# Splitting the last third of the modulation product: its gate half is multiplied during the expert routing, and its weights lead the experts' load queue

## The chip, the cores and the metric

The kernel runs on one core of one Trainium2 chip. Its time is the device time of one execution in microseconds (us). Five engines run side by side on the core: PE does the matrix products, DVE and ACT the elementwise work, POOL little here, and SP issues almost all loads from device memory. Each engine takes its instructions strictly in the order in which they were written for it, and waits on semaphores for the others.

## The reference

The kernel computes two transformer blocks over 256 tokens of width 1024 in fp32. What matters here is the first block and its modulation vector, six pieces of 1024 numbers that all come from one small product:

```python
cond = jax.nn.silu(c)                      # (1, 1024)
mod = cond @ mod_w[l] + mod_b[l]           # (1, 6144)
shift1, scale1, gate1, shift2, scale2, gate2 = jnp.split(mod, N_MOD, axis=-1)
h = modulate(rms_norm(x, norm1_g[l]), shift1, scale1)
x = x + gate1[:, None, :] * mixer_sublayer(h, ...)
h = modulate(rms_norm(x, norm2_g[l]), shift2, scale2)
x = x + gate2[:, None, :] * hierarchical_moe(h, ...)
```

`mod_w` is 1024 x 6144, 24 MiB in fp32. `scale2` is needed as soon as the mixer's last product begins (it goes into the router's weights); `gate2` only where the experts' results are added to x. `hierarchical_moe` gives each token two of 32 experts (1024 to 2 x 256 and back to 1024).

## The kernel before, in words

**Loads.** Weights come in chunks of 1 MiB (128 x 2048 fp32), each issued by SP into a slot of a ring. The mixer's ring has six slots (`load`, L264 to 269). The experts' chunks have a queue of their own, `self.order` (L477): 8 blocks of 4 experts, each with 8 chunks `egu` (gate and up) and 4 chunks `edn` (down). `issue` (L280) takes from that queue into the slots of `eslots` in turn: nine (`ring2`), issued at L852 in the mixer's gate product, five (`ring3`) and the mixer's six, issued during its last product, and three (`ring4`) at L996 in the routing. So 23 expert chunks can be on the chip before the experts begin; the next load has to wait until a slot has been read (`weights`, L288, hands the chunks out in the same order).

**The modulation.** `mod` (L491) multiplies one such chunk at a time: `csil`, the 1024 conditions as 8 columns, is spread to 32 columns and is the stationary operand, and the weights stream past, in four strips of 32 output partitions. `modcols` (L525) copies the sums to SBUF on ACT, turns them with PE transposes, and adds the bias on DVE into `modc`, 48 columns of 128. The first third (`mod0`) is multiplied at the start. The middle third (`mod1`) is done on DVE (`modsum`). The last third, `mod2` (scale2 and gate2, 8 chunks, one per block of 128 conditions, W = 512), is multiplied inside the first part of the input projection: `win_a` (L633) calls `self.pump(2)` (L644) for each of its output tiles from the fourth chunk on, and each call issues a load and then the 4 matmuls of that chunk.

**The rest of the path.** Most weights are split in two parts in fp32r on ACT (`whi`, L300) and DVE (`wlo`, L301), and PE multiplies three products of these (L316, L317, L321). After the mixer, `moe` (L930) turns x with transposes (L950), scales it on ACT (L951, `hn`), and finds each token's experts in a chain of small DVE steps (L968 to 985). Two groups of small matmuls (L989 to 992) count the positions, DVE makes the gather matrices `Ph` (L1063), and PE gathers the tokens (L1072) and multiplies them by the first `egu` chunks (L1089). In the middle of the experts there is one runtime branch (`overflow`, L1247), before which SP has to have issued all loads that stand ahead of it.

The order of each engine's instructions is not the order of the source alone: the program is built by a scheduler that simulates the engines and places each instruction when its operands are due, and pools of buffers make a later writer wait for the earlier reader.

Of the kernel before, what the change touches and what calls it, by code (L numbers as in the profile page):

```python
# [13 lines left out]
F32 = mybir.dt.float32  # L14
# [7 lines left out]
P = 128  # L22
T = 256
D = 1024
KD = D // P
# [3 lines left out]
NE = 32  # L29
# [103 lines left out]
def arrange(x, c, mod_w, mod_b, norm1_g, w_in, conv_w, conv_b, igate_b, fgate_b, q_norm_g, kv_norm_g,  # L133
# [10 lines left out]
    a = {}  # L144
# [2 lines left out]
    half = np.concatenate([np.r_[512 * j:512 * j + 512, 1024 + 512 * j:1536 + 512 * j] for j in range(2)])  # L147
    a["mod0"] = mod_w[0][:, half].reshape(4, 2, P, 2, 1024).transpose(3, 0, 2, 1, 4).reshape(8, P, 2048)
    a["mod1"] = mod_w[0][:, 2048:4096].reshape(KD, P, 2048)
    a["mod2"] = mod_w[0][:, 4096:].reshape(KD, P, 2048)  # L150
    tl = _tiles(p1)
    a["win_a"] = _group(tl, 2)
    a["win_v"] = np.concatenate([_kblk(w1[:, 1024 + 512 * j:1536 + 512 * j], 4) for j in range(2)])
# [69 lines left out]
class Prog:  # L223
# [239 lines left out]
    def run(self, stop=None):  # L463
        tc, nc, I = self.tc, self.nc, self.I
        v, a, g, te = nc.vector, nc.scalar, nc.gpsimd, nc.tensor
        es = ExitStack()
        with es:
            keep = self.pool(es, "keep", 1)
            xT = keep.tile([P, KD, T], F32, name="xT")
            self.const(keep, "first", ["c", "modb", "n1"], nc.sync)  # L470
            nc.sync.dma_start(xT, I["xT"].rearrange("p (k t) -> p k t", k=KD))
            self.const(keep, "tab0", ["ident", "ones", "sel32"], nc.sync)
            modc = keep.tile([P, 48], F32, name="modc")
            cols = keep.tile([P, 64], F32, name="cols")
            self.ring = self.pool(es, "ring", RING1)
            self.eslots, self.eloads, self.ahead = [], 0, []
            self.order = [x for b in range(NE // 4 - 1) for x in self.chunks(b)]  # L477
            self.xT, self.modc, self.cols, self.keep = xT, modc, cols, keep
            with ExitStack() as em:
                self.mixer(em)  # L480
                self.dump("x1", xT)
                if stop == 1:
                    return
                self.moe()
            self.dump("x2", xT)
            if stop == 2:
                return
            self.block2()


    def mod(self, t0, W, src, psum, pool, load=None):  # L491

        nc = self.nc
        ps = psum("md", 1)
        kb = 512 // W
        for ch in range(KD // kb):
            w = (load or self.load)(src(ch))
            yield
            for i in range(kb):
                k = ch * kb + i  # L500
                for j in range(4):
                    nc.tensor.matmul(ps[32 * j:32 * j + 32, :W], self.csil[:, k:k + 1].to_broadcast([P, 32]),
                                     w[:, i * 4 * W + j * W:i * 4 * W + (j + 1) * W], start=k == 0, stop=k == KD - 1)
            yield
        self.modcols(ps, t0, W, psum, pool)

    def modsum(self, t0, name, acc, psum, pool):

# [13 lines left out]
            nc.tensor.matmul(ps[32 * j:32 * j + 32, :], self.co("ones", 0, 32), acc[:, j * 512:(j + 1) * 512], start=True, stop=True)  # L522
        self.modcols(ps, t0, 512, psum, pool)

    def modcols(self, ps, t0, W, psum, pool):  # L525
        nc = self.nc
        row = pool.tile([P, 512], F32, name="mrow", tag="yf", bufs=1)
        nc.scalar.copy(row[:, :W], ps[:, :W])
        nq = W // P
        tmp = psum("md", 1)  # L530
        for q in range(nq):
            nc.tensor.transpose(tmp[:, q * P:(q + 1) * P], row[:, q * P:(q + 1) * P], self.co("ident"))
        nc.vector.tensor_tensor(
            out=self.modc[:, t0:t0 + 4 * nq].rearrange("p (j q) -> p q j", q=nq),
            in0=tmp[:, :W].rearrange("p (q j r) -> p q j r", q=nq, j=4)[:, :, :, 0],
            in1=self.co("modb", t0, 4 * nq).rearrange("p (j q) -> p q j", q=nq), op=OP.add)
# [10 lines left out]
    def mixer(self, em):  # L547
        tc, nc, I = self.tc, self.nc, self.I
        v, a, g, te = nc.vector, nc.scalar, nc.gpsimd, nc.tensor
        mm = te.matmul  # L550
        xT, modc, cols = self.xT, self.modc, self.cols
        with ExitStack() as eo:
# [4 lines left out]
            ps = self.pool(eo, "ps1", 1, space=PSUM)  # L557
# [9 lines left out]
            with ExitStack() as ei:  # L567
                pa = self.pool(ei, "pa", 1)
                tm = self.pool(ei, "tm", 2)
# [32 lines left out]
                for j in range(2):  # L602
# [6 lines left out]
                    for i in range(4):  # L609
                        k = 4 * j + i  # L610
# [3 lines left out]
                                               op0=OP.add, op1=OP.subtract)  # L614
                        a.activation(hf[:, k], hf[:, k], AF.Identity, bias=sh[:, i:i + 1])
                macc = pa.tile([P, 2048], F32, name="macc")
                self.later = [self.mod(32, 512, lambda k: I["mod2"][k], psum, tm), self.modsum(16, "mod1", macc, psum, tm)]

                craw = pa.tile([P, 5, T], F32, name="craw", tag="ce")
                krz = [pa.tile([P, T], F32, name=f"krz{i}") for i in range(2)]  # L620
# [6 lines left out]
                def win_a(ch):  # L627
                    w = self.load(I["win_a"][ch]) if ch else w0
                    if ch == 2:
                        self.const(pa, "trig", ["cos", "sin", "cosq", "sinq"], nc.sync)  # L630
                    if ch == 3:
                        self.const(self.keep, "small", ["n2", "cw", "cb", "qg", "kvg", "fg", "n12", "n22", "b2", "pe", "cw2",
                                                        "cb2"], nc.sync)  # L633
                    if ch == 6:
                        self.const(self.keep, "tab", ["ustrict", "sel64", "riota", "iota"], nc.sync)
                        self.const(pa, "wif", ["wif"], nc.sync)
                        self.rows(self.keep, "row1", ["ib", "fb", "bg", "br"])
                        self.const(pa, "tri", ["negu", "cmask"], nc.sync)
                    pp = psum("a", 2)
                    for j in range(2):  # L640
                        n = ch * 2 + j
                        o = pp[:, j * T:(j + 1) * T]
                        if ch > 2:
                            self.pump(2)  # L644
                        self.tile_a(w[:, j * 1024:(j + 1) * 1024], h, [(o, 0, KD)])
                        if n < 5:
                            a.copy(craw[:, n], o)
                            i = n // 3
                            self.sumsq1(parts[i], craw[:, n], n - 3 * i, groups[i][1], tm)
                        elif n == 5:  # L650

                            kr1 = tm.tile([P, T], F32, name="kr1", tag="x", bufs=5)
                            kr2 = tm.tile([P, T], F32, name="kr2", tag="x", bufs=5)
                            lo, up = slice(0, 64), slice(64, 128)
                            for i, r in ((0, lo), (1, up)):
                                v.tensor_tensor(out=kr1[r], in0=o[lo], in1=self.co("cos")[lo], op=OP.mult)
                                v.tensor_tensor(out=kr2[r], in0=o[up], in1=self.co("sin")[up], op=OP.mult)
                                v.tensor_tensor(out=krz[i][r], in0=kr1[r], in1=kr2[r], op=OP.add)
                        else:

                            c = n - 6
                            xp = tm.tile([P, T + 3], F32, name="xp", tag="x", bufs=5)
                            g.memset(xp[:, 0:3], 0.0)
                            a.copy(xp[:, 3:], o)
                            ca = tm.tile([P, T], F32, name="ca", tag="x", bufs=5)
                            a.activation(ca, o, AF.Identity, scale=self.co("cw", 24 + c, 1), bias=self.co("cb", c, 1))
                            for d in range(3):
                                v.scalar_tensor_tensor(out=ca, in0=xp[:, d:d + T], scalar=self.co("cw", d * 8 + c, 1),
                                                       in1=ca, op0=OP.mult, op1=OP.add)
                            th = tm.tile([P, T], F32, name="th", tag="x", bufs=5)  # L670
                            a.activation(th, ca, AF.Tanh, scale=0.5)
                            v.scalar_tensor_tensor(out=conv[:, c], in0=th, scalar=1.0, in1=ca, op0=OP.add, op1=OP.mult)
# [40 lines left out]
                for ch in range(3):  # L713
                    w = self.load(I["uq"][ch])
                    for j in range(4):
                        n = ch * 4 + j
# [14 lines left out]
                w = self.load(I["uk"][0])  # L731
# [6 lines left out]
                w = self.load(I["uv"][0])  # L738
# [13 lines left out]
                for hd in range(8):  # L752
# [5 lines left out]
                    x = self.softmax(S, Pn, sm)  # L758
# [14 lines left out]
                for c in range(2):  # L773
                    outs = [psum("a", 2) for _ in range(2)]
                    for hf2 in range(2):
                        w = self.load(I["win_v"][c * 2 + hf2])
# [33 lines left out]
                for ch in range(4):  # L810
                    w = self.load(I["win_og"][ch])
# [6 lines left out]
                for hd in range(4):  # L818
# [19 lines left out]
                    yf = tm.tile([P, 2, T], F32, name="yf", tag="yf", bufs=1)  # L838
# [9 lines left out]
            for ch in range(8):  # L848
                w = self.load(I["win_og"][4 + ch])
# [78 lines left out]
    def moe(self):  # L928
# [4 lines left out]
        with ExitStack() as eo:  # L933
# [4 lines left out]
            def psum(tag, bufs):  # L938
                return ps.tile([P, 512], F32, name="ps_" + tag, tag=tag, bufs=bufs)
# [6 lines left out]
            for q in range(2):  # L946
                for j in range(2):
                    o = psum("x", 2)
                    for i in range(4):
                        te.transpose(o[:, i * P:(i + 1) * P], xT[:, j * 4 + i, q * P:(q + 1) * P], self.co("ident"))  # L950
                    a.activation(hn[:, q, j * 512:(j + 1) * 512], o, AF.Copy, scale=rsc[:, q:q + 1])  # L951


            def b2(x, n):
# [871 lines left out]
```

## Time and profile before

| | |
|---|---|
| median of 3 runs | 1007.67 us (1006.49 to 1008.81) |
| the profiled execution | 1006.2 us, span 1004.4 us |
| PE busy | 928.5 us, 92% of the span |
| DVE, ACT busy | 604.9 us, 473.3 us |
| read from device memory | 247.49 MB |

The span is from the first to the last instruction in the trace; 1.8 us of the execution lie around it. Averages say little here, since the stages have different limits: the first 88 us, the mixer up to 326 us, the routing from 326 to 344 us, the experts to about 550 us, and the second block. A stretch is read by asking which engine or queue has no idle time in it, and, where none is full, who waited for whom. PE clock 1.00 is 2.4 GHz, 0.50 is 1.2 GHz.

### The profile page before, as it was taken

What the parts mean: (1) busy time and instruction counts of PE and PEld (TensorE: products, weight loads), DVE (VectorE), ACT (ScalarE), POOL (GpSimd) and SP (SyncE); (2) the same over time, 40 slices, a digit from 0 to 9 for tenths busy, and PEclk for the clock granted to TensorE, in tenths of its full rate; (3) what the DMA queues carried; (4) which work ended last, traced back from release to release, by engine and by line L of the source; (5) the groups of instructions that cost most, each with busy time, mean ns of one, the idle gap of its engine ahead of it and who ended that gap; (6) DMA issues with size and microseconds to landing.
All of it is one profiled execution on the core that took longest, in us unless ns stands there. A gap on an engine that the chain in (4) does not pass through costs nothing. (4 is left out here: it accounts for less than half of the span.)

```text
span 1004.4 us, 17784 instructions
## 1 busy us (share of the span) xinstructions
PE 928.5 (92%) x6870; PEld 761.9 (76%) x6870; DVE 604.9 (60%) x1463; ACT 473.3 (47%) x1006; POOL 13.0 (1%) x28
## 2 busy tenths in 40 slices
PE   4899899999999899997698999899998999999995
PEld 2678888999999545443232898788898889999994
DVE  2468699664663524223123884787769687676764
ACT  3546866555443122121112765476754565555553
POOL 0000000000000000000000000000001000000001
PEclk9899899999999799998989999999999999999998
DMA  8977367669558599999989654643245344555501
GB/s 358 408 275 283 123 243 264 248 233 421 223 204 355 196 420 416 413 422 418 418 344 421 250 189 149 250 152 137 92 169 189 126 169 168 193 185 174 205 1 43
DMA packets 37387, 249.76 MB, mean 249 GB/s; under 512 B 4272, under 2 KB 5040, under 8 KB 8368
## 3 DMA queue, kind: packets, MB, share of 16 engines
q1 hardware_dynamic: 37008, 248.01, 64.0%
q8 instruction: 56, 0.92, 0.4%
q10 hardware_dynamic: 288, 0.55, 0.2%
q14 instruction: 35, 0.29, 0.1%
HBM read 247.49 MB, written 1.05 MB: 247 GB/s over the span
## 5 line engine op out<-in xcount | busy, mean ns | idle before, releaser
L301 DVE TENSOR_TENSOR wlo<-w,whi 128x512 fp32r<-128x512 f32 (+2 forms) x426 | 287.9, 683 | 152.8 <-ACT whi L300 137.5
L300 ACT CAST whi<-w 128x512 fp32r<-128x512 f32 (+2 forms) x426 | 257.7, 611 | 253.1 <-PE ps_a L317 195.2
L316 PE MATMUL ps_a<-hh,whi 128*128 128x256 f32 x304 | 79.1, 292 | 4.9 <-ACT hh L612 3.1
L317 PE MATMUL ps_a<-hl,whi 128*128 128x256 f32 x304 | 78.5, 289 | 0.0
L1132 DVE SCALAR_TENSOR_TENSOR xT<-ps_c,modc,xT 128x256 f32<-128x256 f32 x72 | 33.1, 483 | 72.7 <-PE ps_c L1131 72.6
L316 PE MATMUL ps_a<-h4h,whi 128*128 128x256 f32 x304 | 76.1, 283 | 0.2 <-ACT h4h L343 0.2
L317 PE MATMUL ps_a<-h4l,whi 128*128 128x256 f32 x304 | 76.1, 283 | 0.0
L1089 PE MATMUL ps_gu<-w,xg 128*32 128x512 f32 x512 | 68.7, 618 | 6.5 <-issue 6.5
L316 PEld LDWEIGHTS ps_a<-hh,whi 128*128 128x128 f32 x304 | 59.4, 196 | 9.1 <-ACT hh L612 3.3
L316 PE MATMUL ps_a<-h2h,whi 128*128 128x256 f32 x248 | 64.2, 289 | 0.5 <-DVE kn L1509 0.5
L317 PE MATMUL ps_a<-h2l,whi 128*128 128x256 f32 x248 | 63.0, 284 | 0.0
L317 PEld LDWEIGHTS ps_a<-hl,whi 128*128 128x128 f32 x304 | 59.6, 196 | 2.0 <-issue 1.2
L316 PEld LDWEIGHTS ps_a<-h4h,whi 128*128 128x128 f32 x304 | 58.1, 192 | 1.2 <-ACT h4h L343 0.6
L317 PEld LDWEIGHTS ps_a<-h4l,whi 128*128 128x128 f32 x304 | 58.2, 192 | 0.3
L1131 PE MATMUL ps_c<-PT,eo 128*128 128x256 f32 (+1 forms) x144 | 41.9, 410 | 13.1 <-ACT eo L1137 12.1
L1131 PEld LDWEIGHTS ps_c<-PT,eo 128*128 128x128 f32 (+1 forms) x144 | 24.3, 192 | 37.3 <-ACT eo L1137 16.4
L1072 PEld LDWEIGHTS ps_x<-Ph,hn 128*128 128x128 f32 x256 | 34.0, 198 | 22.4 <-issue 17.6
L321 PE MATMUL ps_a<-hh,wlo 128*128 128x256 f32 x304 | 49.9, 288 | 0.3 <-DVE wlo L301 0.3
L316 PEld LDWEIGHTS ps_a<-h2h,whi 128*128 128x128 f32 x248 | 47.4, 191 | 2.9 <-issue 1.8
L321 PE MATMUL ps_a<-h4h,wlo 128*128 128x256 f32 x304 | 48.7, 283 | 0.0
L1077 ACT ACTIVATE xg<-ps_x,modc,cols 128x128 f32<-128x128 f32 x32 | 14.6, 457 | 70.4 <-PE ps_x L1072 60.9
L317 PEld LDWEIGHTS ps_a<-h2l,whi 128*128 128x128 f32 x248 | 47.4, 191 | 0.2 <-issue 0.2
(527 smaller groups left out, 1998.5 us busy)
## 6 DMA issues: line engine op xcount, KB each, us to landing
w<-in_egu_dram SPq DMA_DIRECT2D x66, 1024.0 KB, 18.4
w<-in_edn_dram SPq DMA_DIRECT2D x33, 1024.0 KB, 19.8
w<-in_up_dram SPq DMA_DIRECT2D x22, 1024.0 KB, 4.7
w<-in_w2a_dram SPq DMA_DIRECT2D x20, 1024.0 KB, 6.6
w<-in_mod_dram SPq DMA_DIRECT2D x19, 1024.0 KB, 7.0
w<-in_win_og_dram SPq DMA_DIRECT2D x12, 1024.0 KB, 5.9
w<-in_dn_dram SPq DMA_DIRECT2D x11, 1024.0 KB, 4.8
w<-in_br_dram SPq DMA_DIRECT2D x8, 1024.0 KB, 12.5
```

Of the source, the lines that this page charges most:

```text
L300: nc.scalar.copy(hi, src)
L301: nc.vector.tensor_tensor(out=lo, in0=src, in1=hi.bitcast(F32), op=OP.subtract)
L316: mm(out, hi[:, s], ah[:, k], start=first, stop=False)
L317: mm(out, hi[:, s], al[:, k], start=False, stop=False)
L321: mm(out, lo[:, s], ah[:, k], start=False, stop=last)
L1072: mm(o[:, i * P:(i + 1) * P], hn[:, q, d * P:(d + 1) * P], Phs[b][q], start=q == 0, stop=q == 1)
L1077: a.activation(xgs[0][:, i], o[:, i * P:(i + 1) * P], AF.Identity, scale=ac[:, d:d + 1], bias=modc[:, 24 + d:25 + d])
L1089: mm(gu[32 * j:32 * j + 32], xgs[d // 4][:, d % 4, j * CAP:(j + 1) * CAP], w[:, j * 512:(j + 1) * 512], start=d == 0, stop=d == KD - 1)
L1131: mm(o[:, i * T:(i + 1) * T], eo_[:, (d0 + i) * P:(d0 + i + 1) * P], PT, start=True, stop=True)
L1132: v.scalar_tensor_tensor(out=xT[:, d], in0=o[:, i * T:(i + 1) * T], scalar=g2[:, d:d + 1], in1=xT[:, d], op0=OP.mult, op1=OP.add)
```

## The change

The weights of `mod2` are cut in two. Four chunks with scale2's 1024 columns stay where they were, now two blocks of conditions to a chunk and W = 256. Four chunks `mod3` with gate2's columns become the first four entries of the experts' queue, and are multiplied in `moe` behind the transposes of x, with a sum in one of the two `dn` banks and a row buffer of the experts' `eo` tag.

```diff
-    a["mod2"] = mod_w[0][:, 4096:].reshape(KD, P, 2048)
+    for n, c0 in (("mod2", 4096), ("mod3", 5120)):
+        a[n] = mod_w[0][:, c0:c0 + 1024].reshape(4, 2, P, 1024).transpose(0, 2, 1, 3).reshape(4, P, 2048)
...
-            self.order = [x for b in range(NE // 4 - 1) for x in self.chunks(b)]
+            self.order = [[(lambda w: w, I["mod3"][k])] for k in range(4)]
+            self.order += [x for b in range(NE // 4 - 1) for x in self.chunks(b)]
...
-    def mod(self, t0, W, src, psum, pool, load=None):
+    def mod(self, t0, W, src, psum, pool, load=None, tag="yf", bufs=1):
...
-        row = pool.tile([P, 512], F32, name="mrow", tag="yf", bufs=1)
+        row = pool.tile([P, 512], F32, name="mrow", tag=tag, bufs=bufs)
...
-                self.later = [self.mod(32, 512, lambda k: I["mod2"][k], psum, tm), self.modsum(16, "mod1", macc, psum, tm)]
+                self.later = [self.mod(32, 256, lambda k: I["mod2"][k], psum, tm), self.modsum(16, "mod1", macc, psum, tm)]
...
-                            self.pump(2)
+                            self.pump()
...
                     a.activation(hn[:, q, j * 512:(j + 1) * 512], o, AF.Copy, scale=rsc[:, q:q + 1])
+            for _ in self.mod(40, 256, lambda k: k, lambda *_: psum("dn", 2), tm, lambda _: self.weights(), "eo", 2):
+                pass
```

Line numbers of the changed kernel are 2 higher from its L150 on, 4 higher from the queue and 8 higher behind the new loop. What moves can be seen at three places. On PE in the input projection, where the second group of the last third's matmuls stands (ps_md is their bank, ps_a the projection's), before and now:

```order
L321 MATMUL ps_a<-hh,wlo 128x256 x4
L502 MATMUL ps_md<-w,csil 32x512 x10
L382 MATMUL ps_m<-tab_62,sqs 128x1 x4
L316 MATMUL ps_a<-hh,whi 128x256
L317 MATMUL ps_a<-hl,whi 128x256
```

```order
L323 MATMUL ps_a<-hh,wlo 128x256 x4
L506 MATMUL ps_md<-w,csil 32x256 x10
L384 MATMUL ps_m<-tab_62,sqs 128x1 x4
L506 MATMUL ps_md<-w,csil 32x256
L318 MATMUL ps_a<-hh,whi 128x256
L319 MATMUL ps_a<-hl,whi 128x256
```

The 32 matmuls stay in this stage with half as many columns; they stood in groups of 6, 10, 8 and 8, and stand in groups of 6, 10, 1 and 15.

On PE in the routing (ps_x holds x turned, ps_dn the new sum, ps_c the positions), before and now:

```order
L904 MATMUL ps_m<-tab_62,sq 128x1 x2
L950 MATMUL ps_x<-tab_62,xT 128x128 x16
L989 MATMUL ps_c<-oh,tab 128x32 x2
L991 MATMUL ps_c<-oh,tab_62 128x32
L992 MATMUL ps_c<-oh,tab 128x32
L991 MATMUL ps_c<-oh,tab_62 128x32
L992 MATMUL ps_c<-oh,tab 128x32
L1035 MATMUL ps_c<-M,tab_62 128x32 x2
L1072 MATMUL ps_x<-Ph_3867,hn 128x128 x2
```

```order
L908 MATMUL ps_m<-tab_62,sq 128x1 x2
L954 MATMUL ps_x<-tab_62,xT 128x128 x8
L506 MATMUL ps_dn<-w,csil 32x256 x15
L954 MATMUL ps_x<-tab_62,xT 128x128 x8
L506 MATMUL ps_dn<-w,csil 32x256 x17
L997 MATMUL ps_c<-oh,tab 128x32 x2
L999 MATMUL ps_c<-oh,tab_62 128x32
L1000 MATMUL ps_c<-oh,tab 128x32
L999 MATMUL ps_c<-oh,tab_62 128x32
L1000 MATMUL ps_c<-oh,tab 128x32
L1043 MATMUL ps_c<-M,tab_62 128x32 x2
L536 MATMUL ps_dn<-tab_62,mrow 128x128 x2
```

15 of the new matmuls stand between the two halves of the transposes, 17 between the transposes and the positions, and two transposes of the new row ahead of the gather.

In SP's queue, from the mixer's branch weights (br) to the loads that follow the routing, before and now:

```order
L268 DMA w<-in_br_dram 128x2048
L284 DMA w<-in_egu_dram 128x2048 x8
L284 DMA w<-in_edn_dram 128x2048
L268 DMA w<-in_br_dram 128x2048 x7
L268 DMA w<-in_wo_dram 128x2048 x4
L284 DMA w<-in_egu_dram 128x2048 x2
L250 DMA wr<-in_wr_dram 128x512
L284 DMA w<-in_egu_dram 128x2048
L284 DMA w<-in_edn_dram 128x2048 x3
L284 DMA w<-in_egu_dram 128x2048 x5
L284 DMA w<-in_edn_dram 128x2048 x4
```

```order
L270 DMA w<-in_br_dram 128x2048
L286 DMA w<-in_mod_dram 128x2048 x4
L286 DMA w<-in_egu_dram 128x2048 x5
L270 DMA w<-in_br_dram 128x2048 x7
L270 DMA w<-in_wo_dram 128x2048 x4
L286 DMA w<-in_edn_dram 128x2048 x2
L252 DMA wr<-in_wr_dram 128x512
L286 DMA w<-in_egu_dram 128x2048 x4
L286 DMA w<-in_edn_dram 128x2048 x2
L286 DMA w<-in_egu_dram 128x2048 x7
L286 DMA w<-in_edn_dram 128x2048 x4
```

Four of the nine early slots now hold `mod3`, and every expert chunk stands four places later in the queue.

## Rows read from the trace of the kernel before

**Rows 1.** Head of the page: span, busy time of each engine
```profile
span 1004.4 us, 17784 instructions
PE 928.5 (92%) x6870; PEld 761.9 (76%) x6870; DVE 604.9 (60%) x1463; ACT 473.3 (47%) x1006; POOL 13.0 (1%) x28
```

**Rows 2.** Stretches: length, PE PEld DVE ACT POOL busy, PE clock, DMA share, GB/s
```profile
52.00:88.00 36.00, 36.00 (x294) 27.64 (x292) 26.61 (x68) 18.09 (x38) 0.60 (x6) 1.00 0.81 316
60.00:88.00 28.00, 28.00 (x237) 21.96 (x236) 25.02 (x66) 14.93 (x32) 0.50 (x5) 1.00 0.89 349
88.00:112.00 24.00, 19.02 (x146) 18.06 (x145) 16.07 (x39) 17.98 (x43) 0.20 (x2) 0.92 0.48 173
112.00:176.00 64.00, 63.78 (x376) 56.73 (x375) 57.69 (x137) 43.02 (x106) 0.00 (x0) 0.98 0.59 217
176.00:326.00 150.00, 149.32 (x1235) 147.37 (x1233) 87.59 (x182) 71.24 (x127) 0.00 (x0) 1.00 0.73 281
344.20:466.00 121.80, 118.65 (x822) 58.01 (x820) 39.62 (x105) 25.55 (x60) 0.00 (x0) 0.99 1.01 415
466.00:476.00 10.00, 3.50 (x16) 1.27 (x20) 1.28 (x3) 0.00 (x0) 0.00 (x0) 0.69 1.01 414
```

**Rows 3.** SP's own waits, 476 to 510 us: total, times, longest
```profile
SPq L1247 <- SPq L1247: 20.1, 8, 3.2
```

**Rows 4.** PE lines, 52 to 88 us: busy, mean ns of one, idle before
```profile
L502 PE MATMUL ps_md<-w,csil 128*32 128x512 f32 x64 | 8.9, 598 | 0.0
L532 PE MATMUL ps_md<-tab,mrow 128*128 128x128 f32 x4 | 0.7, 286 | 0.0
```

**Rows 5.** PE in order of time: start, us, line, form, count
```profile
18.34 1.07 PE L502 MATMUL ps_md<-m,csil 128*32 128x256 f32 x16 [1.30 <-DMA m<-in_mod_dram]
...
23.96 1.94 PE L502 MATMUL ps_md<-m,csil 128*32 128x256 f32 x16
...
70.87 1.92 PE L502 MATMUL ps_md<-w,csil 128*32 128x512 f32 x16
72.72 0.39 PE L316 MATMUL ps_a<-hh,whi 128*128 128x256 f32 x1
```

**Rows 6.** DVE lines, 60 to 88 us: what DVE waited for before wlo
```profile
L301 DVE TENSOR_TENSOR wlo<-w,whi 128x512 fp32r<-128x512 f32 (+1 forms) x14 | 9.3, 678 | 1.0 <-ACT whi L300 0.9
```

**Rows 7.** PE's waits, 88 to 112 us
```profile
PE ps_a L316 <- ACT q L728: 2.5, 2, 2.1
PE ps_a L316 <- ACT ca L666: 1.4, 2, 1.0
```

**Rows 8.** Stretches of the routing, as in rows 2
```profile
330.00:343.50 13.50, 10.96 (x46) 8.54 (x47) 8.99 (x57) 3.75 (x8) 0.00 (x0) 0.50 0.17 69
...
332.60:344.20 11.60, 10.49 (x48) 8.06 (x46) 6.84 (x44) 2.36 (x5) 0.00 (x0) 0.53 0.04 10
```

**Rows 9.** The routing in order of time
```profile
326.90 1.07 PE L950 MATMUL ps_x<-tab,xT 128*128 128x128 f32 x8
...
331.43 1.97 PE L950 MATMUL ps_x<-tab,xT 128*128 128x128 f32 x8 [3.45 <-ACT hn L951]
...
333.80 0.22 DVE L973 TENSOR_TENSOR oh<-sc,m 128x64 f32<-128x64 f32 x1
...
336.46 0.22 DVE L993 SCALAR_TENSOR_TENSOR pos<-ps_c,M 128x64 f32<-128x64 f32 x1 [0.79 <-PE ps_c L992]
...
337.42 0.68 DVE L1063 TENSOR_TENSOR Ph<-pos,tab 128x128 f32<-128x128 f32 x3
...
337.85 3.39 PE L1072 MATMUL ps_x<-Ph,hn 128*128 128x128 f32 x12 [0.57 <-DVE Ph L1063]
...
341.17 1.94 PE L1089 MATMUL ps_gu<-w,xg 128*32 128x512 f32 x8
```

**Rows 10.** SP's issues in order of time
```profile
327.11 0.33 SPq L284 DMA_DIRECT2D w<-in_edn_dram  x1
...
343.17 0.33 SPq L284 DMA_DIRECT2D w<-in_edn_dram  x1
```

More of the change, by code (lines that the diff above doesn't have):

```diff
@@ L504, in mod @@
             yield
-        self.modcols(ps, t0, W, psum, pool)
+        self.modcols(ps, t0, W, psum, pool, tag, bufs)
     def modsum(self, t0, name, acc, psum, pool):
@@ L523, in modsum, with modcols @@
         self.modcols(ps, t0, 512, psum, pool)
-    def modcols(self, ps, t0, W, psum, pool):
+    def modcols(self, ps, t0, W, psum, pool, tag="yf", bufs=1):
         nc = self.nc
-        row = pool.tile([P, 512], F32, name="mrow", tag="yf", bufs=1)
+        row = pool.tile([P, 512], F32, name="mrow", tag=tag, bufs=bufs)
         nc.scalar.copy(row[:, :W], ps[:, :W])
```

## The prediction

> **What bounds the kernel now.** I read the head of the page first: PE is busy 92% of the span, DVE 60% [rows 1]. That is an average over stages, so I next read the table of stretches [rows 2], and in it look for what has no idle time. From 52 to 88 us it is PE: 36.00 of 36 us busy at full clock, with the DMA at 0.81. There the last third of the modulation stands, in 64 records (32 matmuls, two records each), busy 8.9 us with no idle time ahead of them [rows 4]. From 88 to 112 us nothing is full; PE waits for short ACT steps [rows 7]. Up to 326 us PE and, between 112 and 176, DVE (57.7 of 64 us) are nearly full, and the DMA is not (0.59 to 0.73). From 344.2 us it is the other way round: the DMA share is 1.01 at 415 GB/s, and from 466 to 476 us PE is busy 3.5 of 10 us because its chunks have not come. At the end of that stretch SP still sits in its branch [rows 3], since it issues every load ahead of it first. So a microsecond saved before the routing moves everything behind it, and in the experts only the start of the full DMA stretch and the bytes in it count.
>
> Between the two lies the routing. The DMA is empty there: share 0.04 from 332.6 to 344.2 us [rows 8], because SP issued the last load for a free slot at 327.11 us and could issue the next only at 343.17 us, when the first gate-and-up chunk had been read [rows 10]. PE runs at 1.2 GHz from 330 to 343.5 us [rows 8], after standing idle from 327.97 to 331.43 us [rows 9].
>
> **The change, part by part.** *Modulation in the first stage.* Sixteen records of 512 columns take 1.85 us from their first start to the next matmul, 70.87 to 72.72 us; sixteen of 256 columns at the same clock take 1.07 us to their last end [rows 5]. The 64 records stay 64, so the stage loses at least 4 x (1.85 - 1.07) = 3.1 us, and at most half of 4 x 1.85, 3.7 us. Two of four transposes of 0.7 us together go too [rows 4], 0.3 us. PE thus has 3.4 to 4.0 us less, of which I take 3.6. It does not all arrive: from 60 to 88 us DVE is busy 25.0 of 28 us [rows 2], so it can be pressed together by 3.0 us at most, while 52 of the 64 records, 2.9 us, lie there; and 0.9 us of its idle time is waiting for the ACT copy that each split needs [rows 6], which comes with PE's pace and need not shrink. I count 3.0 us for the stage (estimate), with 1.0 and 4.0 us as ends. Four loads fewer are issued there; PE had no wait for a DMA in that stretch, so they are worth nothing. Behind it the order of all engines up to the routing is the same but for one exchange on DVE, and the stretches to 326 us hold no transfer that stands at a fixed time, so the 3.0 us should travel on. The waits of 88 to 112 us are a chain of latencies and shift with it.
>
> *The routing on PE.* 32 matmuls of 256 columns come in, 64 records. Fifteen matmuls stand behind the first half of the transposes, in the hole from 327.97 to 331.43 us: 30 records at 1.07 us per 16 are 2.0 us, hidden. The other seventeen, 34 records, stand behind the second half and ahead of the positions. At 2.4 GHz they take 2.3 us, at 1.2 GHz, by the group of 1.94 us [rows 5], 4.1 us. The second transposes would end near 332.5 us at full clock (1.07 us) and ended at 333.4 us at half [rows 9]. So the seventeen end at 334.8 or at 337.5 us. The positions wait for the second choice, ready at 334.0 us. That is a delay of 0.8 us at full clock and of 3.5 us at half. Queued behind it are the position matmuls, the two transposes of the new row, and the gather, and DVE's pos and Ph wait for those. Against it stand two gains: DVE makes Ph right behind pos, where before a copy that waited for PE stood between (pos ends at 336.68, Ph starts at 337.42, 0.7 us), and wherever the clock is up again the 3.39 us of gather and the first 1.94 us of gate and up [rows 9] run faster; 16 records of one form took 1.07 and 1.94 us at the two clocks, so up to 0.45 of these 5.3 us, 2.4 us. The new row's copy and its bias step need nothing that comes late; gate2 is first read at the first scatter.
>
> *The DMA hole.* The four chunks of gate2 have filled four of the 23 slots, so 19 expert chunks are there when the routing starts. Their slots come free as the 32 matmuls go, at about 329, 333, 334 and 335 to 337.5 us, and SP's four next loads wait for just that. They follow directly on the transfers that ended at 332.6 us. 4 x 1.049 MB at 415 GB/s are 10.1 us, to 342.7 us; the hole lasts to 344.2 us. So the 10 us that would otherwise lengthen the full stretch cost nothing, and the stretch can start at most 1.5 us sooner than before, whatever PE gains. The Trainium skill has another rate: DMA: Bandwidth & Descriptors, Specifications, gives about 358 GB/s of HBM per core. By it the refill would take 11.7 us and the gain in the routing would be nil; this trace moved 415 GB/s over 121.8 us [rows 2], so the trace does not agree and the measured rate stands.
>
> The routing is therefore worth between -3.5 us (half clock throughout, nothing won back) and +1.5 us (the hole's limit). I take +0.5 us, nearer to the upper end, since the hole in PE that stood ahead of the fall of the clock is mostly filled, and three gains stand against one delay.
>
> Sum: 3.0 + 0.5 = 3.5 us. The profiled execution took 1006.2 us, 1.8 us more than its span, and would take 1002.7 us. It lies 1.5 us below the median of the runs; off that median, 1007.67 us, the prediction is 1004.2 us. The ends of the terms give 1.0 - 3.5 = 2.5 us lost and 4.0 + 1.5 = 5.5 us won.
>
> **The rivals.** *DVE holds the first stage.* For it: 25.0 of 28 us busy. Against it: PE, not DVE, has no idle time there. Then 1.0 us of the 3.6 arrives; with the routing at nought, 1006.7 us.
>
> *The clock stays up through the routing.* For it: in the trace the clock fell at 330 us, 2 us into PE's only long idle time of the stretch, and 15 matmuls now cover most of that. Against it: 1.4 us of idle time before the second transposes remains. Then the positions come 0.8 us late but all behind them is fast, the stretch is limited by the hole, and 3.0 to 4.0 + 1.5 us are won: about 1002.7 us. The Trainium skill, TensorE: Matmul & The Clock Gate, says in its Part 1 that the throttled clock is the default and that activity releases it. By it the added matmuls favour this rival; the trace agrees in so far as the fall followed an idle PE.
>
> *The hole is not filled, and the time is longer.* The place is SP's queue behind the routing: the four refills stand behind the three ring4 loads, and each waits for its own chunk's last matmul. If they were held until the first gate-and-up chunk is read at 343.17 us, all 10.1 us would fall into the full stretch: 1007.67 - 3.0 + 10.1 = 1014.8 us. It turns into a loss only when the last refill lands more than about 3 us behind 344.2 us, so when its transfer starts after some 344.7 us. Against it: the ring4 loads had been issued by 327.11 us, and even at half clock the last of the matmuls ends at 337.5 us.
>
> *It does not do what it says.* The scheduler may have placed the new work elsewhere; the order shows it where it was meant. What remains is that the orders in the last experts and the second block changed a little, by which I count 1 us either way into the range.
>
> **How the numbers follow.** A measurement of this kernel tells about 0.2%, 2.0 us, from no change: faster is below 1005.65, slower above 1009.7 us. The forecast has 0.58 (of that 0.54 faster, 0.04 same), the clock rival 0.12 (faster), DVE's rival 0.19 (same), the unfilled hole 0.09 (slower), nothing at all 0.02 (same). That is 0.66 faster, 0.25 same, 0.09 slower. The range runs from 1007.67 - 5.5 - 0.6 for the last orders, 1001.6 us, to 1007.6 us, which takes in DVE's rival and leaves out the unfilled hole and a little more.
>
> **What would show it.** The 64 records between 50 and 85 us should be busy some 5 us instead of 8.9, and the projection's end and all that follows up to 326 us lie about 3 us earlier, which is the main step; if PE instead shows new waits for wlo or ACT there, DVE held it. In the routing, the DMA share between the last ring4 load and the first gate and up should be near 1, not 0.04, and four expert loads issued in it. The start of the first L1089 group against the end of the mixer tells the routing's term, and the clock row of that stretch which rival holds. If the full DMA stretch, measured from its own start to the branch, is longer than before, the hole was not filled and the prediction is wrong.

## The result, and the profile after

The changed kernel takes 1017.73 us (median of 4 runs, 1016.43 to 1020.5) against 1007.08 us of the kernel before in the same session: a ratio of 1.0106 (95% interval 1.0086 to 1.0127), 10.7 us slower. The prediction, 1004.2 us and faster, was wrong in sign. The profiled execution is the slowest of the four: 1020.5 us, span 1018.7 us, 14.3 us more than the span of [rows 1].

I read the trace after from front to back, at the places that the prediction named. First the stretches, columns as in [rows 2]:

```profile
52.00:88.00 36.00, 34.30 (x304) 29.27 (x303) 27.93 (x71) 18.78 (x40) 0.70 (x7) 1.00 0.61 231
88.00:112.00 24.00, 19.27 (x144) 18.60 (x145) 16.41 (x40) 18.36 (x44) 0.10 (x1) 0.93 0.39 139
112.00:176.00 64.00, 63.78 (x373) 56.74 (x372) 57.24 (x137) 42.52 (x104) 0.00 (x0) 0.97 0.60 220
330.00:343.50 13.50, 12.24 (x112) 7.88 (x112) 9.24 (x56) 4.92 (x11) 0.00 (x0) 1.00 0.98 380
332.60:344.20 11.60, 11.24 (x103) 7.02 (x96) 6.96 (x44) 3.55 (x8) 0.00 (x0) 1.00 0.99 384
341.91:466.00 124.09, 116.26 (x814) 56.64 (x814) 40.49 (x106) 25.29 (x59) 0.00 (x0) 1.00 1.01 416
```

In the first stage PE now has idle time. In the routing, against [rows 8], the clock stayed at 1.00 and the DMA share is 0.99 instead of 0.04: the hole was filled. The full DMA stretch runs at 416 GB/s (415 before). The last third's records are down from 8.9 us [rows 4], but PE waits from 52 to 88 us, where it had not waited at all (below: the records, then PE's waits, total, times, longest, from 28 to 52 us, where it was 0.7 us before, and from 52 to 88 us):

```profile
L506 PE MATMUL ps_md<-w,csil 128*32 128x256 f32 x64 | 5.5, 384 | 0.0
...
PE ps_md L506 <- DMA w<-in_mod_dram: 2.2, 2, 1.4
...
PE ps_a L318 <- ACT ca L670: 1.5, 2, 1.1
```

The routing in order of time, against [rows 9, 10]:

```profile
327.37 1.93 PE L506 MATMUL ps_dn<-w,csil 128*32 128x256 f32 x30
330.90 1.24 PE L954 MATMUL ps_x<-tab,xT 128*128 128x128 f32 x8 [1.60 <-ACT hn L955]
332.06 2.35 PE L506 MATMUL ps_dn<-w,csil 128*32 128x256 f32 x34
332.71 7.44 SPq L286 DMA_DIRECT2D w<-in_edn_dram  x4
335.90 0.23 DVE L1001 SCALAR_TENSOR_TENSOR pos<-ps_c,M 128x64 f32<-128x64 f32 x1 [1.03 <-PE ps_c L1000]
338.69 1.06 PE L1097 MATMUL ps_gu<-w,xg 128*32 128x512 f32 x8
341.91 2.41 SPq L286 DMA_DIRECT2D w<-in_egu_dram  x2
```

The 30 records lie in the hole that was empty before, the clock does not fall, and the first gate and up starts at 338.69 us, 2.48 us earlier than in [rows 9]. At the middle of the run the change does what was forecast. SP's later issues tell where that turns, first after, then before:

```profile
546.26 0.33 SPq L252 DMA_DIRECT2D tab<-in_tab_dram  x1
564.20 11.01 SPq L270 DMA_DIRECT2D w<-in_w2a_dram  x3
588.07 16.55 SPq L270 DMA_DIRECT2D w<-in_w2v_dram  x4
706.24 29.55 SPq L270 DMA_DIRECT2D w<-in_wp_dram  x4
1013.43 1.81 SPq L1813 DMA_DIRECT2D out_dram<-xm  x4
```

```profile
549.87 0.33 SPq L250 DMA_DIRECT2D tab<-in_tab_dram  x1
556.75 9.93 SPq L268 DMA_DIRECT2D w<-in_w2a_dram  x3
577.76 14.02 SPq L268 DMA_DIRECT2D w<-in_w2v_dram  x4
690.07 31.55 SPq L268 DMA_DIRECT2D w<-in_wp_dram  x4
999.14 1.82 SPq L1805 DMA_DIRECT2D out_dram<-xm  x4
```

The changed kernel is 3.6 us ahead at the table's load, then 7.5, 10.3 and 16.2 us behind at the next weights, and 14.3 behind at the end. SP issues what slots allow, so the first of these says little about PE. On PE the turn is the stretch from its restart behind the experts' branch (L1255, before L1247, [rows 3]) to the last block's first down product, after and before:

```profile
501.97:550.35 48.38, 40.32 (x241) 15.99 (x241) 11.50 (x28) 5.42 (x13) 0.00 (x0) 0.87 0.94 389
```

```profile
504.27:541.38 37.11, 34.50 (x233) 14.21 (x233) 11.14 (x26) 5.52 (x13) 0.81 (x3) 0.96 0.92 380
```

It begins 2.3 us earlier and is 11.3 us longer: 5.45 us more idle time (8.06 against 2.61) and 5.8 us more busy time, part of it at the lower clock (0.87 against 0.96) and about 1 us because one more down chunk (8 records) lies in it. What stands there? PE and one DVE copy in order of time, after and before:

```profile
519.48 0.71 PE L1080 MATMUL ps_x<-Ph,hn 128*128 128x128 f32 x4 [0.53 <-DVE xg L1082]
520.12 1.06 PE L1097 MATMUL ps_gu<-w,xg 128*32 128x512 f32 x8
521.25 0.41 DVE L1082 TENSOR_SCALAR xg<-ps_x,cols,modc 128x128 f32<-128x128 f32 x1 [1.83 <-PE ps_gu L1097]
521.72 0.71 PE L1080 MATMUL ps_x<-Ph,hn 128*128 128x128 f32 x4 [0.54 <-DVE xg L1082]
522.36 1.06 PE L1097 MATMUL ps_gu<-w,xg 128*32 128x512 f32 x8
```

```profile
514.16 5.36 PE L1089 MATMUL ps_gu<-w,xg 128*32 128x512 f32 x48
```

Before, six chunks are multiplied in one go, 0.89 us each. After, the next block's gather (L1080) stands between two chunks: its bank waits for the DVE copy `xg`, the copy waits until the chunk before has been read, and the chunk behind waits for the gather in PE's order: 2.24 us per chunk. Of these, 0.64 us are the gather (519.48 to 520.12 us), which the kernel before has elsewhere, so some 0.7 us per chunk are lost here (estimate: 2.24 - 0.89 - 0.64). No wait for a transfer is in this. It is the scheduler's order. Between the two kernels 151 of the 212 PE instructions of the experts behind the branch stand at another place, and 669 of 3058 in block 2, although every one of these instructions is the same in both. In the experts ahead of the branch 195 of 439 do, too.

### The profile page after: what moved, and what is told of

Its sections match the earlier page's. It is cut to its first block, busy times and chain, and to the rows that moved or that the text cites. A ratio compares the mean times of both kernels' runs of the same rounds, so it can differ in the third digit from the quotient of the medians.

```text
span 1018.7 us, 17911 instructions
## 1 busy us (share of the span) xinstructions
PE 935.1 (92%) x6934; PEld 764.6 (75%) x6934; DVE 604.5 (59%) x1464; ACT 473.6 (46%) x1007; POOL 13.0 (1%) x28
## 4 chain that ended last, share of the span: by engine, by line
PE 45%; DVE 3%; ACT 1%; DMA 1%; issue 0%; ACTq 0%; DVEq 0%
PE ps_a L318 9%; PE ps_a L319 9%; PE ps_a L323 9%; PE ps_acc L1792 6%; PE ps_gu L1097 1%; PE ps_c L1139 1%; DMA tab<-in_tab_dram 1%; PE ps_t L1563 1%; PE ps_dn L1156 1%; DVE wlo L303 1%; PE ps_y L1567 1%; PE ps_a L340 1%; PE ps_a L342 1%; PE ps_a L341 1%; PE ps_s L1556 1%; PE ps_a L1495 1%
## 5 line engine op out<-in xcount | busy, mean ns | idle before, releaser
L1080 PEld LDWEIGHTS ps_x<-Ph,hn 128*128 128x128 f32 x256 | 34.3, 196 | 32.6 <-issue 14.5
L1139 PE MATMUL ps_c<-PT,eo 128*128 128x256 f32 (+1 forms) x144 | 44.1, 425 | 14.5 <-ACT eo L1145 13.4
```

What stands on the lines that cost most here:

```text
L1080: mm(o[:, i * P:(i + 1) * P], hn[:, q, d * P:(d + 1) * P], Phs[b][q], start=q == 0, stop=q == 1)
L1139: mm(o[:, i * T:(i + 1) * T], eo_[:, (d0 + i) * P:(d0 + i + 1) * P], PT, start=True, stop=True)
```

## The experiments

All ratios are to the kernel before, run on the same chip; 0.1% is 1.0 us.

**e1 to e4: the order behind the branch.** The instructions behind the branch are the same in both kernels, so the order of one can be given to the other: a table lists them by number for each engine, and an edge without a wait ties each to the one ahead. In the changed kernel (e1, e3, e4, e5) the table holds SP's loads too, of which 3 of 90 stand elsewhere; in the kernel before (e2, e6) it holds PE, ACT and DVE only.

```diff
         Prog(tc, I, O).run()
+        pin(tc, ORDER)
...
+def pin(tc, table):
+    for n in numbers(table):
+        i = ins[n]
+        if i.engine in last:
+            tc.add_manual_dep(i, last[i.engine].name, NOSYNC, reason="pin")
+        last[i.engine] = i
```

e1, changed kernel, order of before. 

> The changed kernel, all of its work kept, but behind the experts' branch (experts of the last three blocks, block 2) every engine issues its instructions in the order of the kernel before. Theory A (the order on PE, ACT and DVE behind the branch cost the time; first stage, routing and transfers gained): the 3.6 us by which it leads at 546 us stay to the end, so 1007.1 - 3.6 = 1003.5 us (1002 to 1005). Rival B (four more chunks through the experts' slots put the later chunks and block 2's weights into other slots that come free later; the order only follows from it): it stays slow, 1013 to 1018 us.

 Measured: 1006.91 us, ratio 1.0002 (0.9987 to 1.0016).

e2, kernel before, order of the changed one. 

> The kernel before, with its modulation and its experts' queue as they were, but behind the experts' branch PE, ACT and DVE issue in the order of the changed kernel. Theory A: it loses what the changed kernel lost there, 3.6 us ahead turned into 10.65 (median) to 14.3 us (profiled run) behind, so 14 to 18 us: 1021 to 1025 us. Rival B: no change, 1006 to 1008 us.

 Measured: 1019.05 us, 1.0123 (1.0091 to 1.0155), 2 us under the range of theory A.

e3 and e4 have two tables, one for the experts behind the branch and one for block 2; e3 takes the first, e4 the second from the kernel before. 

> The changed kernel; only the experts of the last three blocks have the order of the kernel before, block 2 keeps that of the changed one. Theory A: the 11.3 us that the stretch from the branch to the last down product was longer (48.4 against 37.1 us) come back, the rest in block 2 stays: 1017.7 - 11.3 = 1006.4 us (1005 to 1009). Rival B: 1013 to 1018 us. A third way (C): block 2 alone is to blame and the experts' loss is taken up by the wait for block 2's weights: 1015 to 1018 us.

 Measured: 1008.28 us, 1.0024 (1.0007 to 1.0041).

> The changed kernel; only block 2 has the order of the kernel before, the experts behind the branch keep that of the changed one. Theory A: the part of the loss that arose behind the experts comes back, about 6.6 us of 17.9: 1011 us (1009 to 1014). Rival B: 1015 to 1018 us. C (block 2 alone): 1003 to 1006 us.

 Measured: 1013.49 us, 1.0080 (1.0050 to 1.0110).

The order costs the whole of the loss, and it costs it in the kernel before too, in which nothing of the modulation was touched: theory A holds, and B falls as an explanation of the loss. Of the ratio of 1.0106, 0.82% (8.3 us) come back with the experts' order; the 0.26% (2.6 us) with block 2's are not clear of noise, as the intervals of 1.0106 and 1.0080 overlap. The two parts are not independent either: in e4 all PE instructions of block 2 stand as in the kernel before, and yet from its first product to the first store of the output it took 447.9 us against 443.3 before (452.1 in the changed kernel), with a granted clock of 0.83 from 637.2 to 657.2 us, where the kernel before had 1.00 (635.9 to 655.9 us). But e1 missed its number by 3.4 us: with the order of before, the lead should have stayed. Its trace shows where it went, ACT and then PE at the end of the experts:

```profile
547.31 0.91 ACT L1327 ACTIVATE h0h<-xT,cols 128x256 fp32r<-128x256 f32 x2 [4.30 <-PE ps_dn L1159]
549.16 0.91 ACT L1327 ACTIVATE h0h<-xT,cols 128x256 fp32r<-128x256 f32 x2 [0.95 <-DVE xT L1143]
549.98 0.56 ACT L1148 COPY eo<-ps_dn 128x512 f32<-128x512 f32 x1
```

```profile
546.17 1.07 PE L1159 MATMUL ps_dn<-w,aT 128*32 128x512 f32 x8
550.59 2.82 PE L1142 MATMUL ps_c<-PT,eo 128*128 128x256 f32 x8 [3.35 <-ACT eo L1148]
554.08 1.10 PE L1429 MATMUL ps_s<-sq,tab 128*32 128x256 f32 x8 [0.67 <-DVE xT L1143]
```

ACT's first write of block 2 (`h0h`) starts just as the last down product (546.17 + 1.07 us) ends. In the program built, that product's chunk lies at 169856 to 178048 bytes and `h0h` takes 167904 to 176096: the same memory. The slots go round by 23; four chunks more turn the round by four, and the last chunk, which lay in `ring2` before, lies in `ring3`, whose memory block 2 uses first. ACT's last `eo` copy is queued behind `h0h`, PE's last scatter behind that, and after the 3.35 us PE's next eight records take 1.10 us; in the kernel before they took 0.66.

**e5, e6: the slot alone.** Only the sequence in which the last chunks take slots is changed, with the order of before in both.

```diff
-        w = self.eslots[self.eloads % len(self.eslots)].tile(...)
+        at = SLOTS.get(self.eloads, self.eloads % len(self.eslots))
+        w = self.eslots[at].tile(...)
...
+SLOTS = {97: 9, 98: 10, 99: 5, 100: 6, 101: 7, 102: 8}      # e5
+SLOTS = {95: 9, 96: 10, 97: 11, 98: 12}                     # e6
```

> The changed kernel in the order of the kernel before behind the branch (as in the run e1), and the last block's twelve chunks take their slots in another sequence: the two of ring3, which came last, come at the end of the gate-and-up chunks. Theory S (what e1 still lost is a slot: the four added chunks turned the round of 23 slots by four, so the last down chunk lies where block 2 writes its first activations, h0h; that ACT instruction waited 4.3 us until the last down product had ended, with the last eo copy queued behind it and PE idle for 3.35 us): 2.3 us of wait and about 1.1 us of the lower clock behind it go, 1006.9 - 3.4 = 1003.5 us (1002 to 1005). Rival D (the transfers, full until 557 us, hold block 2's start whatever the slot): 1006 to 1007.5 us.

 Measured: 1002.83 us, 0.9955 (0.9938 to 0.9971): faster than both kernels.

> The kernel before in its own order behind the branch; only the last four expert chunks take the four slots of ring3, so that the last one lies where block 2's h0h is written, as in the changed kernel. Theory S: the same wait appears, 2 to 3.5 us: 1008.2 to 1009.7 us. Rival D: no change, 1005.5 to 1007 us.

 Measured: 1010.37 us, 1.0039 (1.0026 to 1.0051). The wait of `h0h` in e5, and in e6, total, times, longest:

```profile
ACT h0h L1331 <- DVE xT L1147: 2.4, 2, 1.3
```

```profile
ACT h0h L1323 <- PE ps_dn L1155: 4.3, 1, 4.3
```

In e5 `h0h` waits only for x, as in the kernel before; in e6 the kernel before has e1's wait, to the tenth of a microsecond. Theory S holds, though e6 lies 0.7 us above its range. So B was right on a second, smaller loss. The changed kernel's own order hid it: there all down products of the last block come ahead of the scatters, and `h0h` waits only for x:

```profile
ACT h0h L1324 <- DVE xT L1140: 0.8, 1, 0.8
```

The kernel before was not run with e5's sequence of slots, so it is not tested whether that sequence alone is worth something there.

**e7, e10: without a table.** e10 has e5's slots and leaves the order to the scheduler; e7 has one rule more.

```diff
+                    if b > TURN + 1:
+                        with tc.issue_after(self.gu.ins):      # the last gate-and-up product of block b
+                            gather(b + 1)
```

> The changed kernel, no order given; only the last block's twelve chunks take their slots in the sequence of the run e5. The scheduler, left free, then places 133 of 3124 PE instructions of block 2 otherwise than in the kernel before, where the changed kernel had 669; in the experts behind the branch it is still the changed kernel's order (147 and 151 of 146 to 151 differ). Theory R (the turned round of slots is the root of what block 2 lost: the wait for h0h's memory, and the other order that the scheduler made of it): of 1017.7 us the 4.1 us of the slot (e1 against e5) and most of the 4.2 us of block 2's order (e4) come back, the experts' order stays: 1009 to 1011 us. Rival (the scheduler had placed around the slot already, and block 2's order is another matter): 1014 to 1018 us.

 (Block 2 has 3058 PE instructions and the experts behind the branch 212; the other totals in that text are slips.) Measured: 1014.34 us, 1.0079 (1.0050 to 1.0107). Theory R mostly falls: the slots bring block 2's order near that of before, but only 0.27% back, and the intervals of 1.0106 and 1.0079 overlap.

> The changed kernel without any table of the order: behind the branch the gather of the next block is queued on PE behind the last gate-and-up product of the block before it, and the last block takes its slots as in the run e5; block 2 is left to the scheduler. Theory A with S (the gather placed between the gate-and-up products, each waiting for an ACT or DVE copy, cost most of the 11.3 us in the experts): 1004 to 1008 us, as far as block 2's order comes out like that of before. If the gather's place is not what cost the time: 1012 to 1017 us.

 Measured: 1007.04 us, 1.0005 (0.9990 to 1.0020). The rule is the step from e10 to e7, 0.74%, 7.5 us: the gather's place, with what the scheduler then moved around it, is what cost most. In the two profiles the stretch from PE's restart to the last block's first down product differs by 4.5 us (44.57 against 40.12), so the size is less sure than the sign. From e7 to e5 another 0.5% is in the rest of the order: in e7 125 of the 212 PE instructions in the experts and 133 in block 2 still stand elsewhere than in the kernel before.

**e8, e9: the two stages of the forecast.** e8 queues the new product behind the positions:

```diff
-            for _ in self.mod(40, 256, ...): pass
...
+            with tc.issue_after(at.ins):               # at: the last position matmul
+                for _ in self.mod(40, 256, ...): pass
```

> The changed kernel; the 32 matmuls of the second half of the modulation are queued behind the position matmuls instead of between the transposes. Read from the trace up to 350 us only. Theory K (the routing gained because PE stayed busy and so at full clock): PE stands idle for 3 us and more ahead of the second transposes, its granted clock falls to 0.5 from about 330 us, and the next load for a gate-and-up slot is issued at 344 to 346 us instead of 341.9. Rival (the gain at that load came from the stage before or the filled DMA hole, not from the clock): 341.5 to 342.5 us.

 Measured, one run: the load at 346.92 us. The stretch and PE:

```profile
330.00:343.50 13.50, 12.55 (x102) 9.00 (x102) 6.02 (x34) 3.35 (x7) 0.00 (x0) 0.62 0.51 187
```

```profile
330.52 1.97 PE L954 MATMUL ps_x<-tab,xT 128*128 128x128 f32 x8 [3.46 <-ACT hn L955]
...
335.46 6.16 PE L506 MATMUL ps_dn<-w,csil 128*32 128x256 f32 x64
343.70 1.06 PE L1098 MATMUL ps_gu<-w,xg 128*32 128x512 f32 x8
```

The hole and the fall of the clock of [rows 8, 9] are back: theory K holds on the clock. The Trainium skill, TensorE: Matmul & The Clock Gate, Part 1, has the throttled clock as the default, which activity releases. By that rule the 30 records in the hole are what kept 1.00 here, and the traces agree: 0.62 in this stretch without them, 1.00 with them. The price, 5.0 us at the load, is not that of the clock alone: all 64 records now stand behind the positions and ahead of the gather (6.16 us); in the changed kernel 30 lay in the hole and 34 behind it (2.35 us).

e9 thins the first half of the modulation:

```diff
                 k = ch * kb + i
+                if t0 == 32 and 0 < k < KD - 1:
+                    continue
```

> The changed kernel; of the 32 matmuls of the first half of the modulation only the first and the last k are multiplied, 8 in all (the rest of that product is left out; its loads and the copies behind it stay). Read from the trace up to 260 us only: the first projection of the latents, at 89.98 us in the kernel before and 88.75 us in the changed one, and the first load of the br weights, at 213.09 and 212.55 us. Theory P (PE still holds the stage; what was saved came through in part): 48 records at 0.067 us, 3.2 us more, so 85.5 to 86.5 and 209.4 to 210 us. Theory V (the stage's ACT and DVE steps, and the mod0 chunks that come late, hold it by now): 88 to 88.75 and 212.2 to 212.7 us.

 Measured, one run: 85.61 us and 209.10 us.

```profile
85.61 0.39 PE L318 MATMUL ps_a<-cnh,whi 128*128 128x256 f32 x1 [0.62 <-ACT ca L672]
...
PE ps_a L318 <- ACT ca L672: 3.1, 4, 1.1
```

My own theory V falls: against the means of the changed kernel's first half (88.19 and 211.90 us, in the table below) 2.6 and 2.8 us come through of the 3.2 us taken, although the waits for `ca` grew to 3.1 us. This one execution also lies 1.8 and 1.6 us below the earliest of the seven (87.45 and 210.66 us). PE's work still sets most of the stage.

## Why the prediction was wrong

The step that failed is the last one of the rivals, "that the orders in the last experts and the second block changed a little, by which I count 1 us either way into the range". I had seen that the orders differ and did not count how much; none of the 0.09 given to a slower time stood for them. They cost 1.04%, 10.5 us (1.0106 to e1's 1.0002). The turned slots, which I had not looked for, cost 0.47%, 4.7 us more once the order is that of before (e1 to e5): I followed the four chunks to the slots that they fill and leave, and not to the end of the round.

The rest can be read where no order differs. Ten traces show the two halves as they are, three with the old first half (before, e2, e6) and seven with the new (after, e1, e3, e4, e5, e7, e10); the mean starts are:

| us, mean | latents' first projection | first br load | first gate and up |
|---|---|---|---|
| old (3) | 90.32 | 213.44 | 341.54 |
| new (7) | 88.19 | 211.90 | 338.05 |
| gained | 2.1 | 1.5 | 3.5 |

The lines of two of these columns, before and after:

```profile
89.98 0.39 PE L316 MATMUL ps_a<-cnh,whi 128*128 128x256 f32 x1 [0.98 <-ACT ca L666]
213.09 0.33 SPq L268 DMA_DIRECT2D w<-in_br_dram  x1
```

```profile
88.75 0.39 PE L318 MATMUL ps_a<-cnh,whi 128*128 128x256 f32 x1 [0.98 <-ACT ca L670]
212.55 0.33 SPq L270 DMA_DIRECT2D w<-in_br_dram  x1
```

The means are of few executions on several chips. On the chip of e1 to e4 the gain is 2.6 us at the latents and 2.5 at the br load, on that of e5 to e7 1.8 and 0.3 us, each against one old execution.

- *First stage, 3.0 us.* The reading that PE holds it was right (e9), the size was not: 2.1 us arrive at 88 us and 1.5 at the br load. Of the 3.6 us that PE has less, 1.5 us (2.4 in e3, e4 and e10) turned into waits for `ca`. The step "so it can be pressed together by 3.0 us at most", said of DVE, looked at the wrong engine: it is an ACT copy that frees PE's bank. The longer wait for the `mod0` chunks is not the change's: e2 and e6, with the old half, have 2.0 us of it, and the last chunk is used at 31.59 to 31.88 us in the old executions and at 31.6 to 31.9 us in the new ones, but for 32.16 us in the profiled run of the changed kernel. Behind the latents' projection the executions spread: to the br load it took 122.4 us in e1 and 124.8 in e5. The granted clock of 112 to 124 us in these two:

```profile
112.00:124.00 12.00, 12.00 (x86) 11.36 (x86) 9.29 (x29) 10.47 (x26) 0.00 (x0) 0.99 0.25 88
```

```profile
112.00:124.00 12.00, 12.00 (x79) 11.64 (x79) 8.02 (x26) 9.40 (x25) 0.00 (x0) 0.83 0.26 89
```

- *Routing, 0.5 us.* From the br load to the first gate and up it took 128.08 to 128.12 us in the three old and 126.14 to 126.16 us in the seven new executions: 2.0 us gained. The clock rival was right here, and the hole's limit of 1.5 us did not apply to PE, whose first chunks had been loaded before the routing. At the branch it does show: from the br load to the first load behind the branch 1.2 us are gained in the mean (293.0 against 294.3 us).
- *The hole, for nothing.* It was filled: share 0.99, and the four loads that wait for the new matmuls were issued from 328.50 to 334.44 us (of the group of four shown above, the last, at 339.82 us, already waits for a gate-and-up chunk). But the full stretch became longer. From the second load that waits for a gate-and-up chunk to the first load behind the branch it took 162.8 us (341.91 to 504.73) against 161.5 (345.51 to 507.05), and in all ten traces 162.4 to 164.6 us in the new ones against 161.5 to 162.0 in the old, 1.9 us more in the mean. By the last sign of the prediction this would mean an unfilled hole, so that sign was wrong. One account is the forecast's own limit: with the transfers full up to the branch, only what the hole had beyond the four chunks' 10.1 us can arrive there. Another is the other order of the experts ahead of the branch, which no run gave back. Neither was tested.
- *The sum of the two, 3.5 us,* is what was measured at 338 us, by luck: two errors of opposite sign. At the first load behind the branch 2.7 us are left of it (505.0 against 507.7 us in the mean). With the old order and an untroubled slot (e5) the change is worth 0.45% (0.29 to 0.62), 4.5 us, inside the forecast's range.
- *The rival on the other side* named a mechanism (refills held until 343.17 us) that did not happen. The slower time came from a stage that the change doesn't touch.

What stays open: why the scheduler's simulation arrived at the other order. For block 2 a part is known: with e5's slots alone (e10), 133 instead of 669 of its PE instructions stand elsewhere, so most of that order followed from the slots. For the experts it stays open; that the loads come at other times in the simulation is likely, and was not tried. Nor is it shown which instructions, of the experts or of block 2, cost the rest between e7 and e5.

## What to carry to other kernels

Where a scheduler writes the order, a local edit is two edits: count how many instructions of each engine change places in the stages that the source doesn't touch, and give that its own term and chance, on both signs. When a queue gets n entries more, follow the round of its slots to the last entry, and look what is next written over that memory. Before a change is thrown away as slower, give it the old order: here the same change was 1.06% slower or 0.45% faster.

## What had not been expected of the hardware

Kernels with the same instructions in the same order up to there, and which all kept PE busy for 8.5 of the 12 us from 100 to 112 us, had a granted clock of 0.99 in one execution and 0.83 in another over the next 12 us. That moves the br load by 2.5 us, more than this change gains in that stage. Whether it is the execution or the chip isn't told apart: e1, e3 and e4 (0.99, 0.91, 0.91) ran on one chip, e5 and e7 (0.83, 0.84) on another. So a stage's gain has to be read from several traces, or from a difference inside each: the 128.1 and 126.15 us of the routing's stretch agreed within 0.04 us.
